# A gate quarter between split and expansion, query pieces asked for earlier, and halves of gated results in own tiles

## The chip, the cores and the metric

The kernel runs on one core of a Trainium2 chip. The metric is device time of one execution in microseconds (us). TensorE is PE in the profile, VectorE DVE, ScalarE ACT, GpSimd POOL; SP (SyncE) is the queue from which nearly all DMAs of this kernel are issued.

## The reference, cut to what matters

Two layers work on 1024 latent tokens and 256 context tokens of width 1024. Layer 0 has differential attention beside multi-head latent attention (MLA), layer 1 a bidirectional mLSTM beside neighbourhood attention on a grid of 16 by 64. Each layer has one input projection, a SiLU gate on what its heads give, and one output projection. What the change touches in layer 0:

```
z = h @ w_in + b_in
q1, q2, k1, k2, v, cq, ckv, k_rope, gate = split_cols(z, EVEN_SPLIT)
qm  = rms_norm(cq, q_norm_g) @ w_uq        # 8 heads, 64 + 32 columns each
kvm = rms_norm(ckv, kv_norm_g) @ w_ukv     # 8 heads, keys 64 and values 64
...
ob = softmax_attention(qm, km, vm, MLA_SCALE)
y  = concat([oa, ob]) * silu(gate)
return y @ w_out
```

The rows `cq` (256 columns), `ckv` (128) and `k_rope` (32) are the compressed rows. In layer 1 each head of neighbourhood attention has its result multiplied with its part of the gate in the same way.

## The kernel before, in words

All matrix products of the stage are made of three fp32r products of high and low parts (`product`, lines 434 to 436: high by high, low by high or high by low), so that one logical product is three matmuls. Ten tiles of 128 tokens are worked in three groups, `TG = [(0, 4), (4, 4), (8, 2)]` (first tile, count): two groups of latent tokens, 512 columns each, and one of context, 256 columns.

The input projection leaves the compressed rows in SBUF (`cz`). `compressed(t0, n)` then makes for a group, in this order:
- the **split**: reciprocal norms, scaled rows, three sets of transposes (L1306) into high and low parts `cq` and `ck` (L1310), and the transposed rotary key (L1314), stored to `s_kr` (L1317);
- the **expansion**: four key products (`tr<-ck,wu`) stored to `s_mk` (L1325), six query products (`tr<-cq,uq`) of which two are rotated, stored to `s_mq` by `stored_parts` (L1338; 64-row pieces for four of them, 16-row pieces for the other two), and one value product for each tile (`tr<-wu,ck` in the program's names), stored to `s_mv` (L1360).

High and low parts for the stores go through `parts`: ACT writes `eh` (L452), DVE writes `el` (L453), two buffers each. Value results and gate results share the tile `e`, two buffers. Expansion results lie in PSUM tiles `tr`, gate results in tiles `mm`, four banks each.

`gate(j)` computes a quarter of the gate: two blocks of 128 gate columns over the three groups, 8 x 3 matmuls for each (block, group); so it has 96 matmuls of 512 columns and 48 of 256. ACT applies SiLU (L1373) into `e`, and SP stores `e` to `s_gate` (L1375). The loop of before calls `compressed` for a group and then, for the first two groups, `gate(g)`; after the loop come `gate(2)` and `gate(3)`. In this stretch the framework itself orders the instructions of every engine by a simulated timeline, starting from the program's order; the program decides which tile gets which buffer.

Then comes attention of layer 0, in which a planner (`Plan`) fixes the order by hand: tasks with costs and buffers are put into engine queues, each at the earliest start in a modelled time. It takes tasks in the order in which they were added, within a depth. `Latent.shifts` finds the row maxima of MLA scores, two tiles (128 tokens each) from each query piece: `load_q` (L850) brings a piece of 256 tokens into one of five tiles `rq`, `cut` makes the scores (L858), a maximum is taken (L867). Its keys come by L844 and L845 (`whi`, `wlo`). These steps are spread between those of differential attention, whose scores are L612 and L613, operands `o` loaded by L590 to L592, 12 DMAs to each tile.

Neighbourhood attention in layer 1 is planned in the same way. For a pair of heads with two halves `hf`, `values` writes into a PSUM tile `tp` (L2444), `gated` multiplies it with the gate into a tile `nyy` (L2452), and `store` writes half of it to `s_y`. Before, one `nyy` tile of 1024 columns serves a pair of heads; there is one buffer of it, taken at the first product of a pair and given back at its last store.

Of the kernel before, what the change touches and what calls it, by code (L numbers as in the profile page):

```python
# [11 lines left out]
F32 = mybir.dt.float32  # L12
# [7 lines left out]
P = 128  # L20
D = 1024
KT = D // P
NLAT = 1024
# [31 lines left out]
RQ = 5  # L55
# [146 lines left out]
def hybrid_kernel(ctx, tc, t, out, dbg=None):  # L202
    nc = tc.nc
    V, S, G, T = nc.vector, nc.scalar, nc.gpsimd, nc.tensor
    dma = nc.sync.dma_start
# [22 lines left out]
    s_y = dram.tile([KT, P, NT], F32, name="s_y")  # L228
# [323 lines left out]
                self.load_scores(pool, b)  # L552
            self.load_values(pool)

    spare, stored = {}, []

    def moves(plan, bank, dst, m, last, cut=3):

# [251 lines left out]
    class Latent(Unit):  # L810
# [26 lines left out]
        def shifts(self, plan, a):  # L837


            x = {}  # L840

            def load(_):
                x["k"] = ring[0].tile([P, KT, WC], FR, name=("whi", "wlo")[a]).rearrange("p k n -> p (k n)")[:, :NT]
                dma(out=x["k"][0:64, :].bitcast(F32), in_=s_mk[0][self.p, 64 * a:64 * a + 64, :])  # L844
                dma(out=x["k"][64:96, :].bitcast(F32), in_=s_kr[0])  # L845

            def load_q(i):
                def emit(_):
                    x["q", i] = rough.tile([P, 256], FR, name="rq", bufs=RQ)
                    dma(out=x["q", i][0:96, :].bitcast(F32), in_=s_mq[0][2 * self.p + a][:, i * 256:(i + 1) * 256])  # L850
                return emit

            def cut(tt, c0, k0, n0, nn):
                def emit(_):
                    if c0 + n0 == 0:
                        x["s", tt] = taken("s")
                    s = x["s", tt if tt < LT else LT]
                    T.matmul(s[:, c0 + n0:c0 + n0 + nn], x["q", tt // 2][0:96, tt % 2 * P:tt % 2 * P + P],  # L858
                             x["k"][0:96, k0 * P + n0:k0 * P + n0 + nn], start=True, stop=True)
                return emit  # L860

            def top(tt, n):
                def emit(_):
                    if self.kept is None:
                        self.kept = at.tile([P, 2, TILES], F32, name="kept", bufs=2)
                    w = keys_of(tt)[1]
                    V.tensor_reduce(out=self.kept[:, a, tt:tt + n], in_=x["s", tt][:, :n * w].rearrange("p (m k) -> p m k", k=w),  # L867
                                    axis=AX.X, op=ALU.max, negate=True)
                    given("s", x["s", tt])
                return emit  # L870

# [12 lines left out]
            def loading():  # L884
                x["ready"] = plan.add("D", 2.5, load, [], [f"r{a}"], rank=0)

            def step(tt, n):
                k0, w = keys_of(tt)
                if tt % 2 == 0:
                    x["loaded", tt // 2] = plan.add("D", 0.6, load_q(tt // 2), [], ["rq"], rank=0)  # L890
                last = [x["ready"], x["loaded", tt // 2]]
                cuts = [(tt + i, i * w, k0, n0, nn) for i in range(n) for n0, nn in key_cuts(w)]
                for i, c in enumerate(cuts):
                    freed = [f"r{a}"] * (tt + n == TILES) + ["rq"] * (n == 2 or tt % 2)
                    last = [plan.add("P", c[-1] / 2250, cut(*c), last, [] if i else ["s"],
                                     freed if i == len(cuts) - 1 else [], rank=-2e4 if i else RM)]
                self.shift.append(plan.add("V", on_vector(n * w), top(tt, n), last, [], ["s"], rank=RM))
                if tt + n == TILES and a == 1:
                    last = plan.add("P", 0.2, turn, self.shift, ["tp"])
                    last = plan.add("A", on_scalar(P, False), rows, [last], ["yd"], ["tp"])  # L900
                    self.rows = plan.add("D", 1.0, store, [last], [], ["yd"])
            return loading, [partial(step, tt, 1) for tt in range(LT)] + [partial(step, LT, 2)]

        def scores(self, plan, g):
# [150 lines left out]
    with space(name="pa", bufs=1) as pa, space(name="psa", bufs=1, space=PSUM) as psa0, ExitStack() as wa_stack:  # L1055
# [76 lines left out]
        with space(name="za", bufs=2) as za:  # L1132
# [111 lines left out]
            with space(name="cp", bufs=1, side="right") as cp:  # L1244
# [40 lines left out]
                def compressed(t0, n):  # L1285
# [29 lines left out]
                    pr = parts(za, ps[0:32, :n * P], 32, n * P)  # L1315
                    for i in range(2):
                        dma(out=s_kr[i][:, sl], in_=pr[i])  # L1317
                    for p in range(4):
                        ps = pst.tile([P, 512], F32, name="tr")
                        wsl = slice(p * P, (p + 1) * P)  # L1320
                        product(ps[:, :n * P], lambda k: wk[0][:, wsl], lambda k: wk[1][:, wsl],
                                lambda k: ck[0][:, :n * P], lambda k: ck[1][:, :n * P], 1)
                        pr = parts(za, ps[:, :n * P], P, n * P)
                        for i in range(2):
                            dma(out=s_mk[i][p, :, sl], in_=pr[i])  # L1325
# [36 lines left out]
                def gate(j):  # L1362
                    hi, lo = next(w0)
                    for a in range(2):
                        f = 2 * j + a
                        for t0, n in TG:
                            sl = slice(t0 * P, (t0 + n) * P)
                            ps = psa.tile([P, 512], F32, name="mm")
                            product(ps[:, :n * P], lambda k: hi[:, k, a * P:(a + 1) * P],
                                    lambda k: lo[:, k, a * P:(a + 1) * P],  # L1370
                                    lambda k: hhi[:, k, sl], lambda k: hlo[:, k, sl])
                            e = za.tile([P, 512], F32, name="e")
                            S.activation(out=e[:, :n * P], in_=ps[:, :n * P], func=AF.Silu,  # L1373
                                         bias=vt[0][:, V0["eg"] + f:V0["eg"] + f + 1])
                            dma(out=s_gate[f, :, sl], in_=e[:, :n * P])  # L1375

                for g, tg in enumerate(TG):
                    compressed(*tg)
                    if g < 2:
                        gate(g)  # L1380
            gate(2)
            a0 = attn_stack.enter_context(space(name="a0", bufs=1, side="right"))
            units = [Differential(h) for h in range(4)] + [Latent(p) for p in range(4)]
# [9 lines left out]
    with space(name="a1", bufs=1, side="right") as a1, space(name="at", bufs=1, side="right") as at, \  # L1393
# [67 lines left out]

        loaded(da[1])
        ahead = [u.shifts(plan, a) for u in mla for a in range(2)]
        for loading, _ in ahead[:2]:
            loading()
        parts_left = [(j, step) for j, (_, steps) in enumerate(ahead) for step in steps]
# [752 lines left out]
    with space(name="nf", bufs=1, side="right") as nf, space(name="psf", bufs=1, space=PSUM) as psf:  # L2219
# [98 lines left out]
        def cells(x, hf, g):  # L2318
            return x.rearrange("p (f r g c) -> p f r g c", f=2, r=8, g=4)[:, hf, :, g, :]

        class Neighbours:
# [43 lines left out]
            def plan(self, plan, hf, g):  # L2365
# [79 lines left out]
                    given("npt", x["pt"])  # L2445

                def gated(_):
                    if hf == 0 and g == 1 and a == 0:
                        self.shared["y"] = nf.tile([P, NLAT], F32, name="nyy", bufs=1)
                    self.yy = yy = self.shared["y"]  # L2450
                    for b in range(2):
                        V.tensor_tensor(out=cells(yy, hf, g - 1 + b)[ws],  # L2452
                                        in0=x["o"][64 * b:64 * b + 64, :P].rearrange("p (r c) -> p r c", c=16),
                                        in1=cells(self.gate, hf, g - 1 + b)[ws], op=ALU.mult)
                    given("tp", x["o"])

                def store(_):
                    dma(out=s_y[4 + p, ws, hf * 512:(hf + 1) * 512], in_=self.yy[ws, hf * 512:(hf + 1) * 512])

                o = plan.add("P", 1.36, values, moved, ["tp"], ["npt"])  # L2460
                self.last = plan.add("V", 0.42, gated, [o], ["nyy"] if (a, hf, g) == (0, 0, 1) else [],
                                     ["tp"] + (["unit"] if hf and g == 3 else []), rank=0)
                if g == 3:
                    self.last = plan.add("D", 0.5, store, [self.last], [], ["nyy"] if a and hf else [], rank=1)

        plan = Plan("neighbours", s=2, tp=2, mm=2, np=4, npt=2, eo=2, e=2, hv=2, raw=1, wr=1, unit=2, kl=1, bt0=1, bt1=1, slot=0, y=2, nyy=1)
        manual = ctx.enter_context(ExitStack())
        manual.enter_context(tc.manual_schedule(engines=MANUAL))
        units = [Neighbours(h) for h in range(8)]
# [129 lines left out]
```

## Time and profile before

| | us |
|---|---|
| median of 3 runs | 1875.75 |
| lowest and highest | 1870.58, 1878.41 |
| the profiled execution | 1871.5 |
| its span | 1869.8 |
| mean granted clock | 0.978 of full |

The page has each engine's busy time, slices of the span, the chain of work that ended last, and the costliest groups. A wait is written `engine line <- engine line: sum, times, longest`: what stood, and whose result ended the wait. The timeline gives start and duration of single instructions in us, with the wait ahead of an instruction in brackets; `x8` at an issue in SP's queue (`SPq`) means eight DMAs of that kind in a row, and the duration is that of all of them.

### The profile page before, as it was taken

The page shows a single profiled execution, that of the slowest core. Times are in us where ns is not written, and L with a number is a line of the kernel's source. Part 1 is how long each engine was busy: PE and PEld are TensorE (multiplying, and loading weights), DVE is VectorE, ACT ScalarE, POOL GpSimd, SP SyncE. Part 2 cuts the span into 40 slices and gives each one's busy share as a digit, 9 for nine tenths or more (in the row PEclk, how much of TensorE's full clock was granted, in tenths as well). Part 3 has the DMA queues.
Part 4 walks back from the last instruction along what each step waited for, and adds up shares of the span by engine and source line. Part 5 has one row for each costly group of instructions (what it writes and reads, how often), then busy time and mean ns, then how long its engine had stood idle before and what let it go on. Part 6 is the DMA issues. An engine that isn't in the chain of part 4 may idle for free.

```text
span 1869.8 us, 28148 instructions
## 1 busy us (share of the span) xinstructions
PE 1740.1 (93%) x10354; PEld 1433.9 (77%) x10354; DVE 1107.1 (59%) x1952; ACT 728.9 (39%) x1471; POOL 590.6 (32%) x536
## 2 busy tenths in 40 slices
PE   6999997998988899999989989998999989998898
PEld 4878996787877786566567879887899867776786
DVE  3743224212988887778868743755776125667855
ACT  2422132323766664345523122325553234444521
POOL 1422242111334436567534422210120002223543
PEclk9999999999999999999999989999999999999999
DMA  9777315559426616245163342227432386667651
GB/s 347 230 237 261 115 55 152 165 169 230 109 61 146 137 58 145 78 103 151 59 212 124 108 143 73 90 72 209 161 116 86 106 231 142 179 174 202 196 154 79
DMA packets 203697, 274.19 MB, mean 147 GB/s; under 512 B 21256, under 2 KB 155160, under 8 KB 203304
## 3 DMA queue, kind: packets, MB, share of 16 engines
q1 hardware_dynamic: 203560, 272.39, 50.1%
q8 instruction: 82, 1.34, 0.3%
q14 instruction: 55, 0.45, 0.1%
HBM read 195.33 MB, written 77.00 MB: 146 GB/s over the span
## 4 chain that ended last, share of the span: by engine, by line
PE 67%; DVE 11%; DMA 9%; issue 4%; SPq 4%; ACT 3%; POOL 2%; DVEq 0%; POOLq 0%; ACTq 0%
PE mm L434 8%; PE mm L436 8%; PE mm L435 8%; PE tp L952 4%; PE mm L2011 3%; PE mm L2012 3%; PE mm L2013 3%; PE tp L650 2%; SPq L1338 2%; PE st L916 2%; PE st L918 2%; PE st L917 2%; DVE nm L1402 2%; PE s L858 2%; PE s L612 1%
## 5 line engine op out<-in xcount | busy, mean ns | idle before, releaser
L391 POOL TENSOR_TENSOR wlo<-raw,whi 128x1024 fp32r<-128x1024 f32 (+2 forms) x40 | 97.7, 2444 | 326.0 <-ACT whi L383 322.7
L1402 DVE TENSOR_REDUCE nm<-s 128x1 f32<-128x1280 f32 x64 | 94.2, 1488 | 64.5 <-PE s L613 63.5
L434 PE MATMUL mm<-hhi,whi 128*128 128x512 f32 (+1 forms) x352 | 124.1, 354 | 2.3 <-ACT e L1373 1.4
L436 PE MATMUL mm<-hhi,wlo 128*128 128x512 f32 (+1 forms) x352 | 123.6, 352 | 0.3 <-POOL wlo L391 0.3
L435 PE MATMUL mm<-hlo,whi 128*128 128x512 f32 (+1 forms) x352 | 123.7, 352 | 0.0
L867 DVE TENSOR_REDUCE kept<-s 128x1 f32<-128x1280 f32 (+1 forms) x72 | 100.5, 1395 | 16.2 <-PE s L858 14.9
L383 ACT CAST whi<-raw 128x1024 fp32r<-128x1024 f32 (+2 forms) x54 | 55.9, 1035 | 133.1 <-PE mm L436 53.6
L2401 POOL TENSOR_SCALAR np<-np,nrz 128x640 f32<-128x640 f32 x64 | 53.6, 839 | 168.8 <-DVE nrz L2398 153.6
L1409 ACT ACTIVATE p<-s,nm 128x1280 f32<-128x1280 f32 x64 | 84.9, 1328 | 27.3 <-DVE nm L1402 24.0
L612 PE MATMUL s<-o 128*128 128x512 f32 (+1 forms) x192 | 73.6, 384 | 14.1 <-ACT p L1409 8.3
L2011 PE MATMUL mm<-h,whi 128*128 128x512 f32 x192 | 78.1, 407 | 3.2 <-DVE hv L2047 3.2
L635 POOL TENSOR_SCALAR p<-p,ratio 128x512 f32<-128x512 f32 x32 | 31.9, 998 | 151.1 <-DVE ratio L627 135.7
L650 PE MATMUL tp<-v,pt 128*128 128x128 f32 x640 | 76.9, 277 | 0.9 <-ACT pt L564 0.9
L434 PEld LDWEIGHTS mm<-hhi,whi 128*128 128x128 f32 x352 | 66.6, 190 | 12.9 <-ACT e L1373 1.8
L650 PEld LDWEIGHTS tp<-v,pt 128*128 128x128 f32 x640 | 74.8, 194 | 1.8 <-ACT pt L564 1.4
L932 ACT ACTIVATE pt<-st 128x512 f32<-128x512 f32 (+1 forms) x88 | 50.4, 578 | 66.0 <-PE st L918 57.3
L2012 PE MATMUL mm<-h,whi 128*128 128x512 f32 x192 | 75.7, 394 | 0.0
L2013 PE MATMUL mm<-h,wlo 128*128 128x512 f32 x192 | 75.5, 393 | 0.0
L2394 ACT ACTIVATE np<-np,nnm 128x640 f32<-128x640 f32 x64 | 52.9, 827 | 56.2 <-DVE nnm L2388 49.2
L436 PEld LDWEIGHTS mm<-hhi,wlo 128*128 128x128 f32 x352 | 66.7, 189 | 9.8 <-POOL wlo L391 0.5
L435 PEld LDWEIGHTS mm<-hlo,whi 128*128 128x128 f32 x352 | 66.9, 190 | 9.1
L434 PE MATMUL mm<-whi,hhi 128*128 128x256 f32 (+1 forms) x240 | 73.6, 307 | 0.0
(470 smaller groups left out, 5331.0 us busy)
## 6 DMA issues: line engine op xcount, KB each, us to landing
adaw<-in_ada_w_dram SPq DMA_DIRECT2D x16, 1024.0 KB
raw<-in_od_w_in_dram SPq DMA_DIRECT2D x32, 512.0 KB
o<-s_qk SPq DMA_DIRECT2D x96, 160.0 KB
bt<-in_bias_tables_dram SPq DMA_DIRECT2D x16, 576.0 KB
adaw<-in_ada_dram SPq DMA_DIRECT2D x16, 512.0 KB
o<-s_mq SPq DMA_DIRECT2D x16, 480.0 KB
raw<-in_ev_w_in_dram SPq DMA_DIRECT2D x12, 512.0 KB
s_gate<-e SPq DMA_DIRECT2D x24, 256.0 KB
```

What stands on the lines that cost most here:

```text
L391: (eng or self.eng).tensor_tensor(out=lo, in0=self.raw, in1=hi, op=ALU.subtract)
L434: T.matmul(ps, ahi(k), bhi(k), start=k == k0, stop=False)
L435: T.matmul(ps, ahi(k), blo(k), start=False, stop=False)
L436: T.matmul(ps, alo(k), bhi(k), start=False, stop=k == nk - 1)
L612: T.matmul(s[:, n0:n0 + nn], ql, self.kh[b][:, ks], start=True, stop=False)
L650: T.matmul(o[:, :P], x["pt"][:, c, :], self.v[:, k0 + c, :], start=c == 0, stop=c == nch - 1)
L867: V.tensor_reduce(out=self.kept[:, a, tt:tt + n], in_=x["s", tt][:, :n * w].rearrange("p (m k) -> p m k", k=w), axis=AX.X, op=ALU.max, neg ...
L1402: V.tensor_reduce(out=nm, in_=s[:, :w], axis=AX.X, op=ALU.max, negate=True)
L1409: S.activation(out=p[:, :w], in_=s[:, :w], func=AF.Exp, bias=nm, accum_out=z)
L2011: T.matmul(ps, ah, bh, start=k == 0, stop=False)
L2012: T.matmul(ps, ah, bl, start=False, stop=False)
L2013: T.matmul(ps, al, bh, start=False, stop=k == KT - 1)
```

## The change

Nothing of the computation changes, and no matmul, copy or DMA is added; three orders or buffers do.

1. `compressed` ends after the split and returns `cq`, `ck`; the rest becomes `expanded`. For groups 0 and 1 the loop calls the gate quarter between the two; group 2 has none between.

```
-                for g, tg in enumerate(TG):
-                    compressed(*tg)
+                    c = compressed(*tg)
                     if g < 2:
                         gate(g)
+                    expanded(*tg, *c)
             gate(2)
```

2. Query pieces: the load of a piece was added by the step that uses it first. Now the first five are asked for when the planning begins, and each later one when an odd tile (the second of a piece) or the context step is planned, five pieces ahead of use.

```
+            def asking(i):
+                x["loaded", i] = plan.add("D", 0.6, load_q(i), [], ["rq"], rank=0)
...
-                if tt % 2 == 0:
-                    x["loaded", tt // 2] = plan.add("D", 0.6, load_q(tt // 2), [], ["rq"], rank=0)
+                if (tt % 2 or n == 2) and asked:
+                    asked.pop(0)()
...
+            asked.extend(partial(asking, i) for i in range(5))
...
         ahead = [u.shifts(plan, a) for u in mla for a in range(2)]
+        for ask in asked[:RQ]:
+            ask()
+        del asked[:RQ]
```

3. `nyy` becomes a tile of 512 columns for each half of each head's result, two buffers, taken at `g == 1` and given back by the store of that half.

```
-                    if hf == 0 and g == 1 and a == 0:
-                        self.shared["y"] = nf.tile([P, NLAT], F32, name="nyy", bufs=1)
-                    self.yy = yy = self.shared["y"]
+                    if g == 1:
+                        self.yy = nf.tile([P, 512], F32, name="nyy", bufs=2)
+                    yy = self.yy.rearrange("p (r g c) -> p r g c", r=8, g=4)
...
-                self.last = plan.add("V", 0.42, gated, [o], ["nyy"] if (a, hf, g) == (0, 0, 1) else [],
+                self.last = plan.add("V", 0.42, gated, [o], ["nyy"] if g == 1 else [],
...
-                    self.last = plan.add("D", 0.5, store, [self.last], [], ["nyy"] if a and hf else [], rank=1)
+                    self.last = plan.add("D", 0.5, store, [self.last], [], ["nyy"], rank=1)
```

What the first item does to PE's order around the first key product of group 0 (`tr<-ck,wu`; `mm<-h,w` are gate products). Before:

```order
L434 MATMUL mm<-hhi,whi 128x512
L435 MATMUL mm<-hlo,whi 128x512
L1314 MATMUL tr<-cst,cz 32x128 x4
L434 MATMUL tr<-ck_2548,wu_2171 128x512
L435 MATMUL tr<-ck_2549,wu_2171 128x512
L436 MATMUL tr<-ck_2548,wu_2172 128x512
```

After, in front of the same product:

```order
L436 MATMUL mm<-hhi,wlo 128x256
L434 MATMUL mm<-hhi,whi 128x256
L435 MATMUL mm<-hlo,whi 128x256
L436 MATMUL mm<-hhi,wlo 128x256
L434 MATMUL tr<-ck_2548,wu_2171 128x512
L435 MATMUL tr<-ck_2549,wu_2171 128x512
L436 MATMUL tr<-ck_2548,wu_2172 128x512
```

Before, 35 gate products stand ahead of the first key product, and the others follow between the expansion's; after, all 144 of the quarter do, its products of 256 columns last.

SP's queue at the same place, from the first `s_kr` store to the first `s_mq` store (L1317 is L1321 after, L1325 L1333, L1338 L1346, L1375 L1383). Before:

```order
L1317 DMA s_kr_74<-eh 32x512
L1325 DMA s_mk_72<-eh 128x512
L1317 DMA s_kr_75<-el 32x512
L1325 DMA s_mk_73<-el 128x512
L1325 DMA s_mk_72<-eh 128x512
L363 DMA raw<-in_ev_w_in_dram 128x4x256
L1325 DMA s_mk_72<-eh 128x512
L1325 DMA s_mk_73<-el 128x512 x2
L1325 DMA s_mk_72<-eh 128x512
L1325 DMA s_mk_73<-el 128x512
L1338 DMA s_mq_70<-eh 64x512 x2
```

After:

```order
L1383 DMA s_gate<-e 128x512
L1321 DMA s_kr_74<-eh 32x512
L1321 DMA s_kr_75<-el 32x512
L363 DMA raw<-in_ev_w_in_dram 128x4x256
L1383 DMA s_gate<-e 128x512
L1383 DMA s_gate<-e 128x256
L1383 DMA s_gate<-e 128x512 x2
L1383 DMA s_gate<-e 128x256
L1333 DMA s_mk_72<-eh 128x512 x2
L1333 DMA s_mk_73<-el 128x512 x2
```

The six gate stores of the quarter moved from behind the query stores of group 0 to ahead of its key stores. In group 2 the six gate stores that stood among the key and query stores are gone from there.

The second item in SP's queue, within differential attention of the third head (`o` its score operands, `v` and `gt` values and gate). Before:

```order
L592 DMA o_5008<-s_qk_66 32x1280
L844 DMA wlo<-s_mk_72 64x1280
L845 DMA wlo<-s_kr_74 32x1280
L850 DMA rq<-s_mq_70 96x256
L597 DMA v<-s_v 128x10x128
L599 DMA gt<-s_gate 128x1280
```

After:

```order
L592 DMA o_5016<-s_qk_66 32x1280
L850 DMA rq<-s_mq_70 96x256
L844 DMA wlo<-s_mk_72 64x1280
L845 DMA wlo<-s_kr_74 32x1280
L597 DMA v<-s_v 128x10x128
L599 DMA gt<-s_gate 128x1280
```

The rows read alike, but the piece of a position is now five further on. Elsewhere in attention and in neighbourhood attention the engines' instructions stand in the order of before.

More of the change, by code (lines that the diff above doesn't have):

```diff
@@ L553, in load @@
             self.load_values(pool)
-    spare, stored = {}, []
+    spare, stored, asked = {}, [], []
     def moves(plan, bank, dst, m, last, cut=3):
@@ L1317, in compressed, with expanded @@
                         dma(out=s_kr[i][:, sl], in_=pr[i])
+                    return cq, ck
+                def expanded(t0, n, cq, ck):
+                    sl = slice(t0 * P, (t0 + n) * P)
                     for p in range(4):
@@ L2447, in gated @@
                 def gated(_):
-                    if hf == 0 and g == 1 and a == 0:
-                        self.shared["y"] = nf.tile([P, NLAT], F32, name="nyy", bufs=1)
-                    self.yy = yy = self.shared["y"]
+                    if g == 1:
+                        self.yy = nf.tile([P, 512], F32, name="nyy", bufs=2)
+                    yy = self.yy.rearrange("p (r g c) -> p r g c", r=8, g=4)
                     for b in range(2):
-                        V.tensor_tensor(out=cells(yy, hf, g - 1 + b)[ws],
+                        V.tensor_tensor(out=yy[ws, :, g - 1 + b, :],
                                         in0=x["o"][64 * b:64 * b + 64, :P].rearrange("p (r c) -> p r c", c=16),
@@ L2457, in store @@
                 def store(_):
-                    dma(out=s_y[4 + p, ws, hf * 512:(hf + 1) * 512], in_=self.yy[ws, hf * 512:(hf + 1) * 512])
+                    dma(out=s_y[4 + p, ws, hf * 512:(hf + 1) * 512], in_=self.yy[ws, :])
                 o = plan.add("P", 1.36, values, moved, ["tp"], ["npt"])
-                self.last = plan.add("V", 0.42, gated, [o], ["nyy"] if (a, hf, g) == (0, 0, 1) else [],
+                self.last = plan.add("V", 0.42, gated, [o], ["nyy"] if g == 1 else [],
                                      ["tp"] + (["unit"] if hf and g == 3 else []), rank=0)
                 if g == 3:
-                    self.last = plan.add("D", 0.5, store, [self.last], [], ["nyy"] if a and hf else [], rank=1)
-        plan = Plan("neighbours", s=2, tp=2, mm=2, np=4, npt=2, eo=2, e=2, hv=2, raw=1, wr=1, unit=2, kl=1, bt0=1, bt1=1, slot=0, y=2, nyy=1)
+                    self.last = plan.add("D", 0.5, store, [self.last], [], ["nyy"], rank=1)
+        plan = Plan("neighbours", s=2, tp=2, mm=2, np=4, npt=2, eo=2, e=2, hv=2, raw=1, wr=1, unit=2, kl=1, bt0=1, bt1=1, slot=0, y=2, nyy=2)
         manual = ctx.enter_context(ExitStack())
```

## The prediction

> **What bounds the kernel now.** I began with the page: one engine is nearly always busy.
>
> ```profile
> span 1869.8 us, 28148 instructions
> PE 1740.1 (93%) x10354; PEld 1433.9 (77%) x10354; DVE 1107.1 (59%) x1952; ACT 728.9 (39%) x1471; POOL 590.6 (32%) x536
> ```
>
> TensorE is idle for about 130 us in all, so the question is which of that idle time lies in the three places that the change touches. The first place is the stretch from the MLA split to the first attention score. The busy time of the engines in windows of 20 us (PE, PEld, DVE, ACT, POOL, then the granted clock, the DMA share and GB/s) shows where PE stands still there.
>
> ```profile
> 290.00:310.00 20.00, 20.00 (x99) 16.77 (x98) 8.98 (x13) 6.41 (x12) 2.55 (x2) 1.00 0.85 227
> 310.00:330.00 20.00, 10.09 (x42) 7.15 (x41) 6.10 (x9) 5.20 (x9) 0.00 (x0) 0.79 0.49 142
> 330.00:350.00 20.00, 20.00 (x96) 16.75 (x95) 6.74 (x8) 9.44 (x15) 5.37 (x3) 0.95 0.61 193
> 370.00:390.00 20.00, 16.89 (x96) 15.22 (x96) 4.83 (x11) 8.98 (x19) 2.38 (x1) 0.83 0.66 216
> 410.00:430.00 20.00, 17.52 (x89) 14.26 (x87) 0.00 (x0) 5.69 (x8) 4.74 (x2) 1.00 1.01 269
> ```
>
> Half of 310 to 330 us is lost, and 3 us at the start of group 2. PE's waits there (sum, times, longest) name what it stood for:
>
> ```profile
> PE tr L434 <- DVE el L453: 7.8, 2, 6.7
> PE tr L434 <- DVE e L447: 2.2, 1, 2.2
> PE tr L1306 <- DVE cq L1310: 2.0, 2, 1.1
> PE mm L434 <- ACT e L1373: 1.4, 1, 1.4
> PE mm L434 <- ACT whi L383: 0.9, 1, 0.9
> PE s L612 <- ACT e L1373: 0.6, 1, 0.6
> PE mm L436 <- POOL wlo L391: 0.3, 1, 0.3
> ```
>
> VectorE is only 30% busy at 310 to 330, so `el` is not late for want of VectorE. The chain of waits says what held it:
>
> ```profile
> 309.33 0.53 SPq L1338
> ...
> 323.99 1.67 DMA s_mq<-el
> 325.95 0.70 DVE el L453
> 326.69 0.80 PE tr L434
> ```
>
> The tile `el` has two buffers, and the one that group 1's keys want is free only when the last query store of group 0 has left it. That store stands at the end of a row of stores in SP's queue (start, duration of the issue, count):
>
> ```profile
> 298.85 1.42 SPq L1338 DMA_DIRECT2D s_mq<-eh  x2
> ...
> 320.82 3.60 SPq L1338 DMA_DIRECT2D s_mq<-el  x8
> ...
> 337.77 2.37 SPq L1338 DMA_DIRECT2D s_mq<-el  x2
> 341.19 3.76 SPq L1375 DMA_DIRECT2D s_gate<-e  x2
> 345.33 1.09 SPq L1338 DMA_DIRECT2D s_mq<-eh  x2
> ...
> 370.84 0.90 SPq L1360 DMA_DIRECT2D s_mv<-e  x2
> ...
> 409.88 1.08 SPq L1360 DMA_DIRECT2D s_mv<-e  x2
> ```
>
> Eight stores of 16 rows hold the queue for 3.60 us, 0.45 us each. From 298.85 to 410.96 SP issues expansion stores with few gaps; this row, not PE, sets the stage. The gate products are what PE does beside it.
>
> **Gate quarter between split and expansion.** No product, store or copy is added or removed; the quarter's order against the expansion changes. PE's rows at the places that matter (start, duration, and in brackets the wait):
>
> ```profile
> 278.73 0.48 PE L434 MATMUL mm<-hhi,whi 128*128 128x512 f32 x1
> 279.04 0.39 PE L435 MATMUL mm<-hlo,whi 128*128 128x512 f32 x1
> ...
> 287.13 0.48 PE L434 MATMUL tr<-ck,wu 128*128 128x512 f32 x1
> ...
> 326.69 0.80 PE L434 MATMUL tr<-ck,wu 128*128 128x512 f32 x1 [6.66 <-DVE el L453]
> ...
> 331.13 0.63 PE L435 MATMUL tr<-cq,uq 128*128 128x512 f32 x1
> ...
> 331.97 0.40 PE L434 MATMUL tr<-cq,uq 128*128 128x512 f32 x1
> ...
> 412.93 0.50 PE L434 MATMUL mm<-hhi,whi 128*128 128x512 f32 x1 [1.41 <-ACT e L1373]
> ...
> 450.36 0.28 PE L434 MATMUL mm<-hhi,whi 128*128 128x256 f32 x1
> 450.48 0.28 PE L435 MATMUL mm<-hlo,whi 128*128 128x256 f32 x1
> ...
> 451.49 0.50 PE L612 MATMUL s<-o 128*128 128x512 f32 x1 [0.61 <-ACT e L1373]
> ```
>
> Step 1, the first key product. Before, 35 of the quarter's 96 products of 512 columns run (278.73 to 286.78, 0.23 us each) and then the keys begin at 287.13, with the other gate products between the expansion's. After, the whole quarter stands ahead of the keys: 61 more of 512 columns at 0.23 and 48 of 256 at 0.12 (450.36 to 450.48), 13.9 + 5.7 = 19.6 us. Keys begin near 306.7. The work is not lost, since PE has those products behind it, but SP's row cannot start: it holds only the quarter's own gate stores, six issues, in that time.
>
> Step 2, the row of stores. Group 0's first query store came 11.7 us behind the first key product; I let it come 11.7 to 14 behind, so 318.5 to 320.7 in place of 298.85, and its last 16-row store moves from 324.4 to about 345. Group 1's third key product still waits for the `el` that this store holds: the wait of 6.66 us is not removed but moved to about 348, and the windows between are filled with the same gate products in another place. Group 1's queries have a pause of SP in both orders, behind the gate's `e` tiles (337.77 and 341.19 are two issues each that lasted 2.37 and 3.76). So group 1's values are stored near 392 in place of 370.84, 21 us late.
>
> Step 3, group 2. Here no gate store stands between the expansion's stores any more. From 370.84 to 410.96 SP took 40.1 us; adding up the issues between those two rows I find 32.1 us for the expansion's, 2.0 for six gate stores and 6.0 in gaps. I take away the gate stores and half or more of the gaps: 34.6 us, a gain of 5.5 (2 to 8). The values of group 2 leave at about 426.5, 15.5 us later than before.
>
> Step 4, the end of the stage. In both orders the last 192 gate products follow the last value products and need the `e` tiles that those stores give back: before, PE stood at 412.93 for that and reached the first score at 451.49, 38.6 us later. After, the same 38.6, less 1.2 for two weight waits (0.9 and 0.3) since the last weight block is fetched earlier, plus 2.3: PE will have stood for longer than the 6.66 us after which twelve products took 0.43 us in place of 0.23 (326.69 to 331.97; the row at 331.13 still lasts 0.63 against 0.39). Together 15.5 - 1.2 + 2.3 = **+16.6 us**, between +10 (stores in group 0 closer, gaps of group 2 all gone, no slow clock) and +22 (nothing given back).
>
> The Trainium skill (TensorE: Matmul & The Clock Gate, "What's actually happening") has the array's clock halve after a window of some 3.4 us without work and return after as long a busy one; by it, as an estimate, the slow stretch would cost 1.7 us, and the sum would be +16.0. The trace's stretch was 5.3 us long, so I keep 2.3.
>
> **Query pieces five ahead.** Attention's queries (`rq`, L850) are loaded when the step that needs them is planned; the change asks for them five pieces earlier. What that can save is what PE waited for:
>
> ```profile
> PE s L858 <- DMA rq<-s_mq: 4.5, 2, 3.2
> ...
> 586.67 0.30 SPq L850 DMA_DIRECT2D rq<-s_mq  x1
> ...
> 591.42 1.40 PE L858 MATMUL s<-whi,rq 96*128 96x512 f32 x3 [3.19 <-DMA rq<-s_mq]
> ```
>
> The piece was issued at 586.67, behind twelve loads of `o`, and used 4.75 us later. After, that piece is issued ahead of them. Both waits go, 4.5 us, with nothing due just behind: **-4.5** (0, if the next score waits for ScalarE at the same point, to -6 with the slow clock after the 3.19). The five loads at the head of attention stand in SP's queue between gate stores and the first key loads (L844), so the first `whi` is issued later relative to the first score. The first score of that kind comes some 9 us into attention, and four loads of 0.3 to 0.6 us and one landing fit in that; I cost it at nothing, and price its failure below.
>
> **Halves of gated results.** `nyy` becomes two tiles of half the size for each pair of heads. Instruction orders of the engines in that stage stand as they were; a store now holds a half and the next gated product takes another buffer.
>
> ```profile
> PE tp L2430 <- DVE nyy L2452: 6.7, 4, 5.0
> ```
>
> These four waits name the multiplication that reads the `tp` bank, not the tile it writes: PE wants the bank back. In before only the first halves of a pair of heads had to wait for stores, and those had been issued well before. **0** (-1 to +1; the 6.7 would be the utmost gain if I read the row wrongly, and a store that holds one of the two halves for its 1.7 us of landing the utmost loss).
>
> **The sum.** The profiled execution took 1871.5 us: 1869.8 of span and 1.7 around it. 1871.5 + 16.6 - 4.5 + 0 = 1883.6. The median of the three runs is 1875.75, 4.25 above that execution; the difference of 12 us on the median gives **1887.5 us**, 0.6% slower. About 0.5%, 9.4 us, is what a measurement of this kernel can tell from no change, so the bounds lie at 1866.4 and 1885.1.
>
> **Rivals.**
>
> *SP's row is not the bound, and it is faster.* The place is the same row of stores. If the stores issued close to each other no longer cost 0.45 us each but the 0.3 that a lone one took at 586.67, the 64-row and 16-row stores of the three groups (96 of 16 rows and 48 of 64, 65 us at 0.45) take 20 us less, `el` is back before PE asks, and the gate quarter fills what waiting is left: 7.8 + 2.2 + 2.0 + 1.4 + 0.9 + 0.6 = 14.9 of waits and one slow stretch of 2.3 go, 17 with the 4.5 above at most 22 us: 1854, and with part of it 1860. It decides from the point at which the last value store of group 2 leaves before 410. Against it: every 8-fold issue in the trace lasted 3.6 to 4.0 us, whatever else ran.
>
> The Trainium skill speaks for it (DMA: Bandwidth & Descriptors, "Issuing engines are not separate DMA queues"): the time to start a DMA on a sequencer is usually small beside the DMA itself. By that rule the row would be no bound. The trace differs here: a landing of 1.67 us against 3.60 us of queue for eight. Chance 0.14.
>
> *The row catches up, and nothing can be told.* The pause of SP in group 1 goes: from 337.77 to 345.33 it spent 7.6 us on four issues, which at 0.5 each take 2, so 5.6 are waiting. With group 2 at its upper end (8 in place of 5.5) the stage is 16.6 - 5.6 - 2.5 = 8.5 late, and the query pieces give back 4.5: +4, 1880; without the slow clock and with 6 from the query pieces it is 0, 1876. For it: those are waits of stores on `e`. Against: the order on PE keeps 48 gate products between the two halves of group 1's queries. Chance 0.22.
>
> *The first key loads are late.* Loads of `whi` and `wlo` now stand behind gate stores that wait for the last products. If they land more than 9 us into attention, PE waits at the first L858; a landing as slow as the `rq` one at 586.67 (4.75 us) put behind four issues would cost 3 to 6 and a slow stretch of 2.3: 1893 to 1899. Chance 0.08.
>
> That the change doesn't do what it says is excluded for the gate: the order of after has the quarter ahead of the keys.
>
> **How the numbers follow.** The forecast has 0.56, with its own range 1880 (+10 - 6) to 1898 (+22 + 0). The range 1864 to 1898 leaves out the faster rival and the top of the last one, about 0.18. About a quarter of the forecast's chance lies under 1885.1. Faster: 0.14 and the low edge of the neutral case, 0.16. Same: 0.20 + 0.13 = 0.33. Slower: 0.43 + 0.08 = 0.51.
>
> **What would show it.** Right: the first key product at 305 to 309; the first s_mq store at 318 to 322; a wait on `el` of 5 us or more at 345 to 350; values of group 2 at 424 to 429; the first score at 462 to 474; no wait on `rq` above 1 us. Wrong: a first score before 455, or a last value store within 5 us of 410, would say that SP's row was not what the stage hung on; a first score near 468 with a total that is unchanged would say that the loss is given back later, where I look for nothing.

## The result, and the profile after

| | before | after |
|---|---|---|
| median of 6 runs, us | 1871.87 | 1887.39 |
| lowest and highest | 1866.65, 1878.41 | 1884.52, 1896.24 |
| ratio to before | | 1.0095, 95% interval 1.0077 to 1.0114 |
| span of the profiled execution, us | 1869.8 | 1888.2 |

The change makes the kernel slower, by 15.5 us between the medians and by 18.4 us between the two profiled executions. The windows of 20 us from the MLA split to the first score show where:

```profile
310.00:330.00 20.00, 20.00 (x88) 16.21 (x87) 8.73 (x12) 6.28 (x11) 6.72 (x4) 1.00 0.74 220
330.00:350.00 20.00, 14.84 (x85) 12.38 (x83) 4.83 (x7) 4.76 (x8) 0.00 (x0) 0.93 0.47 106
...
390.00:410.00 20.00, 12.29 (x64) 10.08 (x62) 3.24 (x7) 4.12 (x9) 2.36 (x1) 0.88 0.55 165
410.00:430.00 20.00, 3.29 (x6) 1.66 (x6) 2.39 (x5) 2.21 (x5) 0.00 (x0) 0.50 0.38 97
430.00:450.00 20.00, 19.73 (x86) 16.53 (x87) 0.00 (x0) 3.91 (x7) 0.00 (x0) 0.85 1.00 259
```

The hole of before (310 to 330) is filled; PE now loses 5 us at 330 to 350, and a larger hole has opened at 390 to 430, where PE works 15.6 of 40 us. PE's waits of the stage, in the same form as before:

```profile
PE tr L434 <- DVE el L453: 14.8, 4, 6.3
PE mm L434 <- ACT e L1381: 14.7, 1, 14.7
PE tr L434 <- DVE e L447: 1.1, 2, 0.8
```

The row of stores in SP's queue, at the marks that the prediction set (first query store of group 0, last 16-row store, pause in group 1, values of groups 1 and 2):

```profile
321.23 1.84 SPq L1346 DMA_DIRECT2D s_mq<-eh  x3
...
345.21 3.60 SPq L1346 DMA_DIRECT2D s_mq<-el  x8
...
364.62 3.76 SPq L1383 DMA_DIRECT2D s_gate<-e  x2
368.75 1.09 SPq L1346 DMA_DIRECT2D s_mq<-eh  x2
...
394.26 0.89 SPq L1368 DMA_DIRECT2D s_mv<-e  x2
...
427.15 1.08 SPq L1368 DMA_DIRECT2D s_mv<-e  x2
```

And PE at the first key product, group 1's keys, the last gate products and the first score:

```profile
308.15 0.40 PE L434 MATMUL tr<-ck,wu 128*128 128x512 f32 x1
...
351.10 0.80 PE L434 MATMUL tr<-ck,wu 128*128 128x512 f32 x1 [6.25 <-DVE el L453]
...
430.27 0.79 PE L434 MATMUL mm<-hhi,whi 128*128 128x512 f32 x1 [14.74 <-ACT e L1381]
...
469.76 0.50 PE L612 MATMUL s<-o 128*128 128x512 f32 x1 [0.61 <-ACT e L1381]
```

First key product 21.0 us later than before (287.13), first query store 22.4, values of group 1 23.4, values of group 2 17.3, first score 18.3. Of each of these distances 1.3 us stood there before the stage began, ahead of everything that the change touches. The split's first transposes, before and after:

```profile
277.50 1.47 PE L1306 MATMUL tr<-cst,cz 128*128 128x128 f32 x12
```

```profile
278.80 1.47 PE L1310 MATMUL tr<-cst,cz 128*128 128x128 f32 x12
```

Counted from there the first key product comes 19.7 us later than before, the values of group 2 16.0 and the first score 17.0. The stage holds all but 1.4 us of the 18.4 between the two executions. The longest wait, 14.74 us on the gate tile `e`, ends when one of the last value stores gives that tile back.

In attention the waits on query pieces are gone, but the place of the larger one shows that other waits stood close behind. After:

```profile
607.76 0.85 PE L858 MATMUL s<-whi,rq 96*128 96x512 f32 x3 [0.98 <-ACT p L1418]
611.61 2.50 PE L650 MATMUL tp<-v,pt 128*128 128x128 f32 x20 [0.76 <-DVE yd L793]
614.91 0.63 PE L1435 MATMUL tp<-cst,p 128*128 128x128 f32 x4 [0.80 <-DVE p L638]
```

The score in front of it stood 18.5 us later than before (604.91 against 586.37), this one 16.3 (607.76 against 591.42). Behind the two waits that follow the distance is 16.8 us, and behind a wait on the row maxima `kept`, 1.67 us in place of 1.02, it is 17.4 (620.27 against 602.83).

### The profile page after: what moved, and what is told of

Same layout as the page of the kernel before. It is cut to its first block, busy times and chain, and to the rows that moved or that the text cites. A ratio compares the mean times of both kernels' runs of the same rounds, so it can differ in the third digit from the quotient of the medians.

```text
span 1888.2 us, 28167 instructions
## 1 busy us (share of the span) xinstructions
PE 1744.4 (92%) x10354; PEld 1436.8 (76%) x10354; DVE 1110.6 (59%) x1952; ACT 728.8 (39%) x1471; POOL 591.9 (31%) x536
## 4 chain that ended last, share of the span: by engine, by line
PE 66%; DVE 13%; DMA 8%; SPq 4%; issue 4%; ACT 3%; POOL 2%; DVEq 0%; ACTq 0%; POOLq 0%
PE mm L434 9%; PE mm L435 9%; PE mm L436 9%; PE tp L956 4%; SPq L1346 3%; PE mm L2023 2%; PE mm L2024 2%; PE mm L2025 2%; PE tp L650 2%; PE st L920 2%; PE st L922 2%; PE st L921 2%; DVE nm L1411 2%; PE s L612 1%; PE s L858 1%
## 5 line engine op out<-in xcount | busy, mean ns | idle before, releaser
L612 PE MATMUL s<-o 128*128 128x512 f32 (+1 forms) x192 | 74.7, 390 | 14.7 <-ACT p L1418 8.3
L434 PEld LDWEIGHTS mm<-hhi,whi 128*128 128x128 f32 x352 | 67.0, 191 | 25.5 <-ACT e L1381 15.5
```

What stands on the lines that cost most here:

```text
L434: T.matmul(ps, ahi(k), bhi(k), start=k == k0, stop=False)
L612: T.matmul(s[:, n0:n0 + nn], ql, self.kh[b][:, ks], start=True, stop=False)
```

## The experiments

Theory: the row of store issues in SP's queue sets this stage, it starts 21 us late, and what PE has left behind the last value products comes on top. The rivals are named with each run. Unless said otherwise a run has the query pieces and the halves of the change. "First score" is the first L612 of the profiled execution (451.5 before, 469.8 after), "last values" the last `s_mv` issue (409.9 and 427.2). The profiled executions reach the split's first transposes between 276.3 and 278.8 us, so first scores that lie less than some 2 us apart say something only when they are counted from there: 174.0 us before, 191.0 after.

**Only the gate quarters moved.** Query pieces and halves as before.

```
...
                 for g, tg in enumerate(TG):
-                    compressed(*tg)
+                    c = compressed(*tg)
                     if g < 2:
                         gate(g)
+                    expanded(*tg, *c)
```

> Only the gate quarters are moved between split and expansion; query pieces and the halves of gated results are as before. Theory (the row of SP's stores starts 20 us later and everything behind it moves): the first attention score 17 to 19 us later than before, as with the whole change, and nothing given back in attention, so 18 to 21 us slower than before, 1 to 2 us more than the whole change. Rival (the loss is spread over all three parts): at most 12 us slower.

Measured: 1884.56 us against 1868.9, ratio 1.0087 (1.0064 to 1.0109); first score 468.7, 191.0 counted from the split as with the whole change. The moved quarters alone make the loss, 16 us; the expected size (18 to 21) was 2 us too large, and nothing is to be had from the other parts.

**Everything but the moved quarters.**

```
-                    if g < 2:
-                        gate(g)
                     expanded(*tg, *c)
+                    if g < 2:
+                        gate(g)
```

> The gate quarters stand behind the expansion as before; query pieces five ahead and halves of gated results as in the change. Theory: the stage up to attention is as before; the two waits on query pieces (4.5 us) go, but only 1 to 2 us arrive at the end, since another wait stands close behind; halves cost nothing: 0 to 2 us faster than before. Rival (query pieces give what the waits held): 4 to 5 us faster. Rival (halves or the early pieces cost something): slower by 1 us or more.

Measured: ratio 1.0003 (0.9988 to 1.0018); first score 174.1 us behind the split, 174.0 before. The 4.5 us of waits on query pieces are worth nothing that can be told; the halves cost nothing.

**The quarter between split and expansion in one group only.** Group 0 alone, then group 1 alone (with 0 and 1 exchanged):

```
-                    if g < 2:
+                    if g == 0:
                         gate(g)
                     expanded(*tg, *c)
+                    if g == 1:
+                        gate(g)
```

> The whole change, but the quarter stands between split and expansion in group 0 alone; group 1 has its quarter behind the expansion. In PE's order the first key product stands behind 144 gate products as in the change, but group 1's queries have no gate products between them. Theory (the row of stores is the bound): the row starts 21 to 23 us late as in the change; in group 1 its pause of about 6 us behind the gate tiles goes, and group 2 has gate stores between again, 2 us: 13 to 18 us slower than before, first query store near 321. Rival (each of the two moved quarters costs half, by the waits on the shared tile e): 8 to 10 us slower.

> The whole change, but the quarter stands between split and expansion in group 1 alone; group 0 has it behind the expansion. Theory: the row starts at 299 as before, and group 1's keys stand at 327 as before; but 192 gate products now stand between the two halves of group 1's queries in place of 48, so the row pauses there until about 370 in place of 345: 15 to 25 us slower than before. Rival (what costs is the late first key product of group 0 alone): within 3 us of before. Rival (each quarter costs half): 8 to 10 us slower.

Measured: group 0 alone 1.0053 (1.0035 to 1.0072), first query store at 320.2, first score 459.7; group 1 alone 1.0131 (1.0104 to 1.0159), first score 473.7. Values of group 1, the first pair, in the one and in the other:

```profile
383.05 0.90 SPq L1368 DMA_DIRECT2D s_mv<-e  x2
```

```profile
399.20 0.89 SPq L1368 DMA_DIRECT2D s_mv<-e  x2
```

With group 0 alone the row starts as late as in the change, but without gate products between the halves of group 1's queries its pause goes, and it is 11.2 us ahead of the change (394.26) at this mark, 10.2 counted from the split. I had put that pause at 6 us, so 9.9 us of loss came in place of 13 to 18; the number alone does not tell the theory from "each quarter half". Group 1 alone does: the row starts on time, pauses until 373.8, and costs more than both quarters together (1889.7 to 1899.3 us, against 1881.7 to 1885.0 of the runs with only the two quarters moved). A quarter has no price of its own; what counts is where it stops the row.

**Splits and expansions first, all gate quarters last.**

```
-                    if g < 2:
-                        gate(g)
                     expanded(*tg, *c)
+                gate(0)
+                gate(1)
             gate(2)
```

> All three groups are split and expanded first and all four gate quarters follow (query pieces and halves as in the change). The row of stores has no gate stores within it and no pause: last value store at 390 to 398 in place of 410. Theory (stage = row, then what gate products are left for PE): 480 of the 576 gate products are left, 92 us, so the first score at 480 to 492: 28 to 40 us slower than before. Rival (the row alone sets the end; the first score follows the last value store by 41 us as in the other runs): first score at 431 to 440, 12 to 20 us faster.

Measured: 1913.01 us, ratio 1.0235 (1.0209 to 1.026). The row has no pause and its last values go out 15 us earlier than before:

```profile
394.91 1.09 SPq L1368 DMA_DIRECT2D s_mv<-e  x2
```

Then 480 gate products run from 399.31, and the first score comes at 493.4. The row alone is not the bound either: it must run while PE has gate products to do. The loss, 44 us, is a little over the range.

**Value results in tiles of their own**, so that the gate has `e` to itself:

```
-                        e = za.tile([P, 512], F32, name="e")
+                        e = za.tile([P, 512], F32, name=f"z{i % 2}")
                         evac(e, ps)
                         dma(out=s_mv[(t0 + i) * P:(t0 + i + 1) * P, :], in_=e)
```

> The whole change, but the value results go through the tiles of the rotated queries and no longer through the tile e of the gate. The wait of 14.7 us on e should go. The framework's order then leaves 57 gate products behind the last value product in place of 192. Theory: the row still starts at 320 and ends at 415 to 425; after it come the loads of attention's operands, some 20 us, and no long row of products: first score at 440 to 450, 1 to 11 us faster than before. Rival (the row is no bound and only the shared tile cost): first score at 430 or before.

Measured: 1.0064 (1.0044 to 1.0084), slower than before where I expected faster. The last values went out at 426.3, as in the change. The wait on `e` behind the value products shrank to 9.35 us but did not go. PE had its last gate product at 441, but the first score waited:

```profile
441.04 0.28 PE L436 MATMUL mm<-hhi,wlo 128*128 128x256 f32 x1
462.91 0.80 PE L612 MATMUL s<-o 128*128 128x512 f32 x1 [21.59 <-ACT e L1381]
```

ScalarE could not empty the gate's PSUM banks, since both `e` tiles waited for their stores, and SP's queue holds the 24 loads of attention's operands in front of those:

```profile
427.44 0.95 SPq L1383 DMA_DIRECT2D s_gate<-e  x2
428.50 0.47 SPq L590 DMA_DIRECT2D o<-s_qk  x1
...
446.84 1.14 SPq L1383 DMA_DIRECT2D s_gate<-e  x2
```

ScalarE stood 23.6 us, 15.5 of them before these stores were issued. The rival (only the shared tile cost) falls; the same in-order queue was most of the limit a second time, at a place that I had not counted.

**Fewer issues: all query parts merged.** One store of 128 rows for each product and part:

```
-                            for h in range(P // w):
-                                dma(out=s_mq[b][h0 + h, r0:r0 + w, sl], in_=pr[b][w * h:w * h + w, :])
+                            dma(out=s_mq[b][h0:h0 + P // w, r0:r0 + w, sl], in_=pr[b])
```

In the order of before, and in the order of the change:

> Gate quarters behind the expansion as before (with the query pieces and the halves of the change), and the query parts of a product go to memory by one store of 128 rows in place of two of 64 or eight of 16, so that SP issues 24 stores of queries in the stage in place of 144. Theory (SP's row of issues is the bound): an issue of 128 rows takes 0.35 to 0.6 us, the row shrinks from some 112 us to under 70, the wait on el at 327 goes and PE works through: first score at 430 to 438 in place of 451, 13 to 21 us faster than before. Rival (the queue's time follows the rows or bytes, or el is late for another reason): within 4 us of before.

> The whole change, with the same merged query stores. Theory: with the row no longer the bound, a first key product that comes 20 us later costs nothing, because PE has the same products to do: within 4 us of the same stores in the order of before, so 11 to 21 us faster than before. Rival (the order itself costs, by the tile e that gate and value results share): still 12 us or more slower than the merged stores in the order of before.

Measured: 1936.27 us (1.0368, 1.0343 to 1.0392) and 1945.9 us (1.0407, 1.0383 to 1.0431). Both theory and rival had these wrong by far. The edit leaves 36 query stores and not 24. In the first of the two runs the queue came to take five us for each store of group 1:

```profile
391.29 4.96 SPq L1345 DMA_DIRECT2D s_mq<-eh  x1
396.35 4.95 SPq L1345 DMA_DIRECT2D s_mq<-el  x1
```

256 KB in 4.95 us are 53 GB/s. I took it that an outer dimension of two (two heads of 64 rows) leaves a store with two of the 16 DMA engines, and that one of eight would have eight. The window between supports the first: the DMA share (the last number but one) is 0.13 of 16 engines, that is two.

```profile
391.00:396.00 5.00, 0.65 (x2) 0.56 (x3) 0.69 (x1) 0.00 (x0) 0.00 (x0) 0.50 0.13 51
```

These two runs say nothing of the order of gates.

**Fewer issues: only the 16-row parts merged**, eight stores into one with eight as outer dimension:

```
+                            if w == 16:
+                                dma(out=s_mq[b][:, r0:r0 + w, sl], in_=pr[b])
+                                continue
                             for h in range(P // w):
```

> Gate quarters behind the expansion (query pieces and halves as in the change); only the 16-row query parts are merged, eight stores of 16 rows into one with eight as its outer dimension; the 64-row parts stay two stores. In the run with all parts merged, the stores with two as outer dimension moved at 51 GB/s, a fifth of what the others reach. Theory (SP's row is the bound, and that slow transfer was what broke the merged run): an outer dimension of eight moves at 150 GB/s or more, the row loses 84 of 144 query stores, about 12 us in each of the first two groups, the wait on el at 327 goes: first score at 430 to 440 in place of 451.5, 11 to 21 us faster than before. Rival (el and e are late for another reason): first score within 4 us of before's.

> The whole change with the same merged 16-row parts. Theory: the row starts 21 us late as in the change but is short enough to end before PE is through: first score within 5 us of the same stores in the order of before, 8 to 21 us faster than before. Rival (a late first key product costs by itself): 12 us or more slower than the same stores in the order of before.

Measured: 1858.89 us in the order of before (0.9944, 0.9924 to 0.9964), 1867.46 in that of the change (0.9984, 0.9969 to 0.9998). A merged store holds the queue for 0.58 to 0.87 us, most of them for under 0.66, where eight took 3.60 (order of before):

```profile
309.10 0.65 SPq L1346 DMA_DIRECT2D s_mq<-eh  x1
309.85 0.59 SPq L1346 DMA_DIRECT2D s_mq<-el  x1
```

The wait of 6.66 us on `el` at group 1's keys is gone there and the first score comes at 440.7, 10.8 us earlier than before. The theory's first half holds, at the lower edge of its range (0.7 us outside it by the first score, and 10.5 us by the ratio where at least 11 was expected). Its second half does not: in the order of the change the first score came at 451.4, 10.7 us later than with the same stores in the order of before; within 5 had been expected. The medians differ by 8.6 us, so the rival's 12 is not reached either. The last values show why, first the order of before, then that of the change:

```profile
399.23 1.06 SPq L1371 DMA_DIRECT2D s_mv<-e  x2
```

```profile
408.90 0.80 SPq L1371 DMA_DIRECT2D s_mv<-e  x2
```

The shorter row still ended 9.7 us later, and 192 gate products still stood behind it; the row had not become short enough.

**Two queues.** The high parts of the queries are issued from ScalarE's queue, the low parts from SP's, in the order of before:

```
+                            issue = S.dma_start if b == 0 else dma
                             for h in range(P // w):
-                                dma(out=s_mq[b][h0 + h, r0:r0 + w, sl], in_=pr[b][w * h:w * h + w, :])
+                                issue(out=s_mq[b][h0 + h, r0:r0 + w, sl], in_=pr[b][w * h:w * h + w, :])
```

> Order of before (query pieces and halves as in the change); the high parts of the queries (72 of 144 stores) are issued from ScalarE's queue, the low parts stay on SP. Theory: two queues issue in parallel, SP's row shrinks by some 33 us over the stage, the wait at 327 goes: first score at 432 to 445, 6 to 20 us faster than before; ScalarE is held 30 to 35 us by the issues and the gate's SiLU may wait for it. Rival (the stores are limited by the DMA engines that both queues share): within 4 us of before.

Measured: 1857.86 us, 0.9938 (0.9923 to 0.9953); first score at 436.7, within the range. The two queues issue beside each other:

```profile
309.67 4.24 SPq L1347 DMA_DIRECT2D s_mq<-el  x8
```

```profile
308.01 4.83 ACTq L1347 DMA_DIRECT2D s_mq<-eh  x8
```

Eight stores of 16 rows take 4.1 to 5.7 us in SP's queue and 3.7 to 7.0 in ScalarE's, where most took 3.6 to 3.8 in one queue, so two queues are less than twice as fast. But the waits on `el` are gone, and PE's longest wait in the stage is 2.3 us. The Trainium skill (DMA: Bandwidth & Descriptors, "Issuing engines are not separate DMA queues") states that starting DMAs from several engines saves only the sequencer's time, usually small beside the transfer. The "usually small" does not hold here: a store that landed in 1.67 us stood in a row of eight that held the queue for 3.60, and sharing that time between two queues was worth 11.6 us of the kernel.

**Both remedies in the order of the change.** This is the test that the runs with merged 16-row parts had left open: does the order cost anything once the row is short?

```
+                            issue = (S.dma_start, dma)[b]
+                            if w == 16:
+                                issue(out=s_mq[b][h0:h0 + P // w, r0:r0 + w, sl], in_=pr[b])
+                                continue
...
```

> The whole change, with the high parts of the queries issued from ScalarE's queue and the 16-row parts of both merged, so that SP issues 36 query stores less than a third of what it did and ScalarE as many. In the runs before, the first score followed the last value store by 40 to 43 us whenever 192 gate products stood behind the last values; PE's order of the change has these last values at 389 if PE never waits. Theory (a late start of the row costs only as long as the row is longer than what PE has to do beside it): the last value store at 392 to 400, first score at 433 to 441, as with two queues in the order of before (436.7), 8 to 20 us faster than before. Rival (the order of the change costs some 10 us by itself, as the run with merged 16-row parts alone showed): first score at 445 or later, 2 us faster or less.

Measured: 1859.12 us, 0.9941 (0.9926 to 0.9957); 30 query stores are left in each queue, not 36. First score:

```profile
439.61 0.50 PE L612 MATMUL s<-o 128*128 128x512 f32 x1 [0.61 <-ACT e L1385]
```

In the predicted band, and 30.2 us earlier than with the change and its own stores (469.76). The last value store, at 403.35, is outside its band of 392 to 400, and the first score followed it by 36.3 us and not by 40 to 43. What kept its distance is the start of the last gate products: PE began them at 401.20, and the first score came 38.4 us later, against 38.6 before.

The same order that costs 17 us with 144 query stores in one queue stands within the intervals of the faster kernels of the order of before. Counted from the split its first score comes at 162.3 us, against 160.4 with two queues and 163.6 with merged 16-row parts in that order. So no price of the order by itself can be told here; it has one as long as a row of issues hangs on the expansion. Both remedies together in the order of before were not run, so a price of some 2 us is not excluded. The last three kernels named (16-row parts merged, two queues, both) beat before and after; they cannot be told from each other.

## Why the prediction was right

- **First key product** forecast at 306.7, came at 308.15; **first query store** at 318.5 to 320.7, came at 321.23. Of both delays 1.3 us stood ahead of the stage. Counted from the split, the key product came 19.7 us later than before, where 19.6 had been added up. The step was right: the gate products in front of the keys are not lost work, but hold the row back.
- **The wait on `el`** was forecast as moved, at about 348; it ended at 351.10 with 6.25 us.
- **Group 1's pause** stayed (364.62 to 368.75); its values came 23.4 us late in place of 21, 22.1 counted from the split. Group 0 alone showed that the pause is worth about 10 us, nearly twice what I had put into the neutral rival, but the change keeps it.
- **Group 2**: 34.0 us from the first values of group 1 to the end of the row, 34.6 forecast (40.1 before).
- **First score** +18.3 us, +16.6 forecast; 1.3 us of the difference stood ahead of the stage, and from the split on it is +17.0.
- **Query pieces**: this is the step that failed. "Both waits go, 4.5 us, with nothing due just behind" gave 1.1 us at the end of this stretch, and the run without the moved quarters shows nothing. A wait on the attention weights `p` of 0.98 us took the place of the 3.19, two more, 0.76 and 0.80, follow, and one on `kept` is 0.65 longer. My reading, which no run tests, is that ScalarE, VectorE and PE hang on each other's results there at every step, so that a wait of one is a pause in which the others catch up. The forecast of this term should have been near the lower bound, 0.
- **Halves**: 0, as forecast; PE's waits on that multiplication read 6.1 us in the profile of after (6.7 before).
- **The sum**: the errors of the stage and of the query pieces have one sign, so the medians lie 15.5 us apart and not 12. That the median came within 0.2 us of the forecast is chance: the three runs of before that were known lay 3.9 us above the median of the six, which made up for the 3.5 us that the difference was short.

On the rivals: the faster one was refuted for this kernel, since its eightfold issues lasted 3.5 to 4.6 us again, though its mechanism is real: with the row cut by other means the kernel is 11 us faster. (Its sum took 0.45 us for the 64-row stores too; the rows have two of them in 1.19, 0.59 each.) The neutral one asked for a pause that goes; it stayed. The late key loads did not show: the first L858 waited 1.71 us, for `p`, as before (1.68).

About 1.5 us are lost in attention at one place with the same waits as before (0.90 and 0.46). The granted clock is 0.72 there for 6 us in the profile of after, against 1.00 in that of before:

```profile
700.00:706.00 6.00, 4.64 (x17) 3.51 (x16) 4.43 (x10) 3.61 (x8) 2.70 (x4) 0.72 0.07 18
```

```profile
682.00:688.00 6.00, 4.55 (x25) 3.60 (x26) 5.51 (x11) 4.13 (x10) 2.27 (x5) 1.00 0.00 1
```

What set the clock down there was not tried and stays open.

## What to carry to other kernels

Look for the row of issues in an in-order queue before giving an engine other work to "fill" a wait: filling moves the start of the row, and the wait comes back behind it. A stage of this kind ends with the row's end plus the work that was left behind it, so independent work belongs beside the row, neither ahead of it nor after it. When the queue is what bounds, fewer or split issues gained 11 us here, where orders of the same instructions lost 10 to 44.

## What the runs showed of the hardware that I had not expected

- A store whose DRAM side has an outer dimension of two moves 256 KB in 4.95 us, 53 GB/s, with a DMA share of 0.13. The first two of the stage were issued in 0.59 and 0.53 us; in the row of such stores in group 1 three issues lasted 4.95 or 4.96 us each. With eight as outer dimension an issue took 0.58 to 0.87 us. The Trainium skill (DMA: Bandwidth & Descriptors, "Why a DMA increments its semaphore by 16 and not by 1") says that a DMA runs on the largest number of engines up to 16 that divides the slowest dimension of both sides, which makes two and eight here. For two the run agrees; for eight no run here shows it, since the time of an issue is not that of the transfer. I should have looked there before merging all parts.
- Two queues that issue at once are less than twice as fast as one: eight stores of 16 rows took 4.1 to 5.7 us in SP's and 3.7 to 7.0 in ScalarE's, against 3.5 to 4.9 in one alone, most of them 3.6 to 3.8.
